# The first pieces of k and q of a rotary-embedding score kernel, split over two DMA rings

## The chip, the cores and the metric

The kernel runs on one core of a Trainium2 chip. The metric is the time of the kernel on the device in microseconds (us), the median of the runs shown. The core has TensorE (PE) for matmuls and transposes, VectorE (DVE) and ScalarE (ACT) for elementwise work, GpSimd (POOL), and SyncE (SP), which in this kernel does nothing but issue transfers. Transfers between the large memory (HBM) and the on-chip memory run on 16 DMA engines. SyncE and ScalarE can both issue them, each into a queue of its own; a DMA issue is an instruction on the issuing engine's queue (written SPq, ACTq, POOLq in the profile), and a semaphore tells when the data has landed.

## The reference

The inputs q and k have the shape (16, 512, 16, 64): batch, position, head, dimension. Both are rotated by position, and then every query of a head is multiplied with every key of the same head and batch:

```python
q_rot = concat([q1 * cos - q2 * sin, q1 * sin + q2 * cos], axis=-1)   # q1, q2: halves of the last axis
k_rot = concat([k1 * cos - k2 * sin, k1 * sin + k2 * cos], axis=-1)
scores = einsum('bshd,bthd->bsht', q_rot, k_rot)                      # (16, 512, 16, 512), float32
```

The inputs are 67 MB, the output is 268 MB.

## The kernel before, in words

A batch has 512 positions; position 4p + c lies in partition p, so that a batch of q or k is a tile of 128 partitions x 4 positions x 16 heads x 64 values, 2 MB, loaded by one DMA (`load`, L122). The kernel walks over 64 steps, four a batch. From batch 1 on, a step is one c: its q tile is rotated on VectorE by `rope` (two products, L149 and L150, and a sum, L154), transposed on TensorE through an identity (L170), copied out of PSUM (L185), and multiplied with the batch's transposed keys (`scores`, L201); ScalarE copies each 128 x 1024 result into a stage tile (L208), and one DMA of 4 MB stores the tile (`store`, L188). There are three stage buffers. The order of all instructions is written out by hand under `tc.manual_schedule()`; each engine's queue runs in program order. Batches are loaded well ahead, and the loads stand in SyncE's queue between the stores.

Batch 0 is treated differently, so that work can begin before 2 MB have landed. It is cut by heads: a step of batch 0 is four heads, with all four c. `load_units` loads pieces of it into a tile named `early`: the first four heads of k, then those of q (512 KB each, runs of 1 KB), then the other twelve heads of k and of q (1536 KB each, runs of 3 KB). Their DMAs are issued at L67. Batch 0's results are stored in pieces of 1 MB (L211).

Before these, ScalarE issues the loads of cos and sin (L225, 64 KB each), and then makes `ss_t` out of sin (L232 and L233: a copy, and a copy times -1). The first instruction of ScalarE proper is a table load, which the profile puts on L232. VectorE's first product (L149) needs the first piece of k and `ss_t`, its second (L150) `cos_t`.

Five later loads (`RELIEVED`) go through GpSimd's queue in another split (`load_around`, L98, L111). They are untouched.

The waits between engines and DMAs are set by the framework. DMAs issued by SyncE and ScalarE take turns on eight semaphores, so the ninth DMA waits, before it is issued, until the first has landed.

Of the kernel before, what the change touches and what calls it, by code (L numbers as in the profile page):

```python
# [10 lines left out]
def kernel(  # L11
# [8 lines left out]
    nc = tc.nc  # L20
# [4 lines left out]
    B, S, H, D = q.shape  # L25
    HD = D // 2
    P = 128
# [3 lines left out]
    G = H // C  # L31
# [27 lines left out]
    units = {}  # L59
    used = [0]  # L60

    def load_units(which, head, heads):
        n = C * heads * D
        t = early[:, used[0] : used[0] + n].rearrange("p (c e) -> p c e", c=C)
        used[0] += n
        src = dram[which][0, :, :, head : head + heads, :]
        nc.sync.dma_start(t.rearrange("p c (h d) -> p c h d", d=D), src)  # L67
        for h in range(0, heads, G):
            units[which, (head + h) // G] = t[:, :, D * h : D * (h + G)]

# [42 lines left out]
    def load(which, b):  # L113

        if b >= B:
            return
        t = in_pool.tile([P, C, H * D], fp32, tag=which + "_in", name=which + "_sb")
        batches[which, b] = t
        if (which, b) in RELIEVED:
            load_around(which, b, t)  # L120
        else:
            nc.sync.dma_start(t.rearrange("p c (h d) -> p c h d", h=H), dram[which][b])  # L122

    def rope(which, n):


        part = part_pool.tile([P, H * D], fp32, tag="part", name="part")
        if n < C:
            x = units[which, n]
            sv, k1, k2 = "p c (g j) -> p c g j", {"j": HD}, {"j": D}  # L130
            cs = cos_t.unsqueeze(2).to_broadcast((P, C, 2 * G, HD))
            ss = ss_v.unsqueeze(2).to_broadcast((P, C, G, D))
            pv = part.rearrange("p (c g j) -> p c g j", c=C, j=D)
            x5 = x.rearrange("p c (h x j) -> p c h x j", x=2, j=HD)
            p5 = part.rearrange("p (c h x j) -> p c h x j", c=C, x=2, j=HD)
            adds = [(x5[:, :, :, y], p5[:, :, :, 1 - y]) for y in range(2)]
        else:
            x = batches[which, n // C][:, n % C]
            sv, k1, k2 = "p (g j) -> p g j", {"j": HD}, {"j": D}
            cs = cos_t[:, n % C].unsqueeze(1).to_broadcast((P, 2 * H, HD))  # L140
            ss = ss_v[:, n % C].unsqueeze(1).to_broadcast((P, H, D))
            pv = part.rearrange(sv, **k2)
            x4 = x.rearrange("p (h x j) -> p h x j", x=2, j=HD)
            swapped = bass.AP(part.tensor, part.offset + HD, [part.ap[0], (D, H), (-HD, 2), (1, HD)])
            adds = [(x4, swapped)]
        xs, xc = x.rearrange(sv, **k2), x.rearrange(sv, **k1)

        def products():
            nc.vector.tensor_tensor(pv, xs, ss, op=mult)  # L149
            nc.vector.tensor_tensor(xc, xc, cs, op=mult)  # L150

        def sums():
            for y, z in adds:
                nc.vector.tensor_tensor(y, y, z, op=add)  # L154

        return [products, sums]
# [33 lines left out]
    def scores(i, p, st):  # L190

        ps = ps_s_pool.tile([P, 2, S], fp32, tag="ps_s", name="ps")
        b = i // C
        if b == 0:
            c, hp = divmod(p, 2)
            lhs, rhs = qT[i][:, C * hp + c], kT[0][:, 2 * i + hp]
        else:
            lhs, rhs = qT[i][:, p], kT[b][:, p]
        for r in range(2):
            po, rh = ps[:, r, :], rhs[64 * r : 64 * r + 64, :]  # L200
            nc.tensor.matmul(  # L201
                out=po, lhsT=lhs[64 * r : 64 * r + 64, :], rhs=rh, start=True, stop=True
            )
        so, si = st[:, 2 * p : 2 * p + 2, :], ps
        if b > 0:
            so = so.rearrange("s r (t c) -> s r t c", c=C)
            si = si.rearrange("s r (c t) -> s r t c", c=C)
        nc.scalar.copy(out=so, in_=si)  # L208
        if b == 0 and p % 2 == 1:
            c = p // 2  # L210
            nc.sync.dma_start(o_v[0, c, :, G * i : G * (i + 1)], st[:, G * c : G * (c + 1)])  # L211
        elif b > 0 and p == HP - 1:
            store(i, st)

    def tr_act(which, n):
        for g in range(2):
            transposed(which, n, g, nc.scalar.copy)

    def run(ops):
        for op in ops:  # L220
            op()

    with tc.manual_schedule():
        for t, src in ((cos_t, cos), (sin_t, sin)):
            nc.scalar.dma_start(t, src.rearrange("(p c) j -> p c j", c=C))  # L225
        for head, heads in ((0, G), (G, H - G)):
            load_units("k", head, heads)
            load_units("q", head, heads)
        load("k", 1)
        load("q", 1)  # L230
        make_identity(nc, ident)
        nc.scalar.copy(out=ss_t[:, :, 0, :], in_=sin_t)  # L232
        nc.scalar.mul(ss_t[:, :, 1, :], sin_t, -1.0)  # L233
        for which in ("k", "q"):
            run(rope(which, 0))
            tr_act(which, 0)


        for i in range(C):
            st = st_first[i] if i < 2 else stage_pool.tile([P, H, S], fp32, tag="stage", name="st")  # L240
            if i < C - 1:
                dve = rope("k", i + 1) + rope("q", i + 1) + rope("k", C + i)
                nxt = [("k", i + 1), ("q", i + 1)]
            else:
                dve = rope("q", C) + rope("k", C + i) + rope("q", C + 1) + rope("k", 2 * C)
                nxt = [("q", C), ("k", C + i)]
            for p in range(HP):
                scores(i, p, st)
                if p in (0, 1) and i > 0:
                    run(dve[:1])  # L250
                    dve = dve[1:]
                    transposed("k", C + i - 1, p, nc.vector.tensor_copy)
                if p == 3 and i < 2:
                    load("kq"[i], 2)
                if p in (2, 6):
                    m = len(dve) - (4 if p == 2 else 2) - (2 if i == C - 1 else 0)
                    run(dve[:m])
                    dve = dve[m:]
                    tr_act(*nxt.pop(0))
            run(dve)  # L260
        load("k", 3)


        for i in range(C, NST):
            tr = {}
            if i + 1 < NST:
                tr[1], tr[3] = ("q", i + 1, 0), ("q", i + 1, 1)
            if i + C < NST:
                tr[5], tr[6] = ("k", i + C, 0), ("k", i + C, 1)
            dve = []  # L270
            if i + 2 < NST:
                dve += rope("q", i + 2)
            if i + 1 + C < NST:
                dve += rope("k", i + 1 + C)
            st = stage_pool.tile([P, H, S], fp32, tag="stage", name="st")
            for p in range(HP):
                scores(i, p, st)
                if p not in tr:
                    continue
                if tr[p][0] == "q":  # L280
                    run(dve[:1])
                    dve = dve[1:]
                    transposed(*tr[p], nc.vector.tensor_copy)
                else:
                    transposed(*tr[p], nc.scalar.copy)
            run(dve)
            if i % C == C - 2:
                load("q", i // C + 2)
            elif i % C == C - 1:
                load("k", i // C + 3)  # L290
# [30 lines left out]
```

## Time and profile before

| | |
|---|---|
| time, median of 3 runs | 792.87 us (792.67 to 793.26) |
| profiled execution | span 790.4 us, from the first to the last instruction; no other time of this execution is given |
| PE, DVE, ACT busy | 684.4 us (87%), 544.7 us (69%), 562.0 us (71%) |
| DMA | 336.18 MB, 425 GB/s over the span; SyncE's queue (q1) 325.46 MB, GpSimd's (q0) 10.10 MB, ScalarE's (q10) 0.13 MB |
| first piece of k, issue to landing | 4.8 us |
| first piece of q, issue to landing | 5.6 us |
| sin, issue to landing | 3.7 us |
| 4 MB stores, issue to landing | 24.7 us (median of 60) |
| mean granted TensorE clock | 0.934 |

An engine's busy time is what its instructions took; issuing a DMA isn't counted as busy. The page's rows of 40 digits cut the span into 40 slices and give the busy share in tenths. The time from issue to landing includes the time in which a transfer stands behind others in its queue. A stretch of time is shown by the trace with the busy time of PE, PE's weight loads, DVE, ACT and POOL in it, then the granted clock, the mean busy share of the 16 DMA engines, and GB/s.

### The profile page before, as it was taken

What the parts mean: (1) busy time and instruction counts of PE and PEld (TensorE: products, weight loads), DVE (VectorE), ACT (ScalarE), POOL (GpSimd) and SP (SyncE); (2) the same over time, 40 slices, a digit from 0 to 9 for tenths busy, and PEclk for the clock granted to TensorE, in tenths of its full rate; (3) what the DMA queues carried; (4) which work ended last, traced back from release to release, by engine and by line L of the source; (5) the groups of instructions that cost most, each with busy time, mean ns of one, the idle gap of its engine ahead of it and who ended that gap; (6) DMA issues with size and microseconds to landing.
All of it is one profiled execution on the core that took longest, in us unless ns stands there. A gap on an engine that the chain in (4) does not pass through costs nothing.

```text
span 790.4 us, 7750 instructions
## 1 busy us (share of the span) xinstructions
PE 684.4 (87%) x3072; PEld 296.4 (38%) x3072; DVE 544.7 (69%) x516; ACT 562.0 (71%) x647; POOL 11.9 (2%) x24
## 2 busy tenths in 40 slices
PE   4989998988988889798996989889899798799960
PEld 2444443433433334343342433334334343344420
DVE  6999988666766678576785767667678487587400
ACT  3888886865857768486785866777577586588770
POOL 0000000000001000000000001000000000000000
PEclk9999999998999999898998989999899899899995
DMA  9999999999999999999999999999999999999997
GB/s 357 417 425 439 429 430 435 425 435 436 429 429 428 413 432 419 433 423 438 433 427 436 426 432 429 422 432 424 430 432 427 436 429 432 430 432 434 432 429 340
DMA packets 18836, 336.18 MB, mean 425 GB/s; under 512 B 2312, under 2 KB 3592, under 8 KB 4616
## 3 DMA queue, kind: packets, MB, share of 16 engines
q1 hardware_dynamic: 16704, 325.46, 96.4%
q0 software_dynamic: 1808, 10.10, 3.1%
q8 instruction: 24, 0.39, 0.2%
q10 hardware_dynamic: 288, 0.13, 0.1%
q14 instruction: 12, 0.10, 0.0%
HBM read 67.24 MB, written 268.44 MB: 425 GB/s over the span
## 4 chain that ended last, share of the span: by engine, by line
DMA 49%; PE 40%; ACT 5%; DVE 3%; issue 1%; ACTq 0%; SPq 0%; DVEq 0%
DMA out_dram<-st 46%; PE ps L201 30%; PE bank L170 10%; ACT st L208 5%; DMA q_sb<-in_q_dram 2%; DVE part L149 1%; DMA early<-in_k_dram 1%; DVE q_sb L150 0%; DVE k_sb L154 0%; DVE k_sb L150 0%; DVE q_sb L154 0%; DVE early L150 0%; DVE kT_t L185 0%; ACTq L316 0%; DVE early L154 0%
## 5 line engine op out<-in xcount | busy, mean ns | idle before, releaser
L208 ACT COPY st<-ps 128x1024 f32<-128x1024 f32 x512 | 495.7, 1020 | 192.6 <-DMA out_dram<-st 109.8
L201 PE MATMUL ps<-kT_t,qT_t 64*128 64x512 f32 x2048 | 544.0, 649 | 67.0 <-ACT st L208 67.0
L201 PEld LDWEIGHTS ps<-kT_t,qT_t 64*128 64x128 f32 x2048 | 183.6, 196 | 256.2 <-issue 133.3
L185 DVE COPY qT_t<-bank 128x512 f32<-128x512 f32 x118 | 81.6, 691 | 193.9 <-PE bank L170 193.9
L170 PEld LDWEIGHTS bank<-ident,q_sb 128*128 128x128 f32 x480 | 54.2, 149 | 99.0 <-issue 96.4
L170 PEld LDWEIGHTS bank<-ident,k_sb 128*128 128x128 f32 x480 | 50.3, 140 | 96.4 <-DVE k_sb L150 39.5
L170 PE MATMUL bank<-ident,q_sb 128*128 128x128 f32 x480 | 85.1, 304 | 0.9 <-PE ps L201 0.9
L170 PE MATMUL bank<-ident,k_sb 128*128 128x128 f32 x480 | 78.5, 286 | 1.6 <-DVE qT_t L185 1.2
L185 ACT COPY kT_t<-bank 128x512 f32<-128x512 f32 x122 | 72.4, 598 | 6.4 <-PE bank L170 6.4
L154 DVE TENSOR_TENSOR k_sb<-k_sb,part 128x1024 f32<-128x1024 f32 x60 | 73.5, 1225 | 2.1
L150 DVE TENSOR_TENSOR q_sb<-q_sb,cos_t 128x1024 f32<-128x1024 f32 x60 | 73.5, 1225 | 2.1
L150 DVE TENSOR_TENSOR k_sb<-k_sb,cos_t 128x1024 f32<-128x1024 f32 x60 | 73.5, 1225 | 2.0
L149 DVE TENSOR_TENSOR part<-q_sb,ss_t 128x1024 f32<-128x1024 f32 x60 | 73.5, 1225 | 2.0
L149 DVE TENSOR_TENSOR part<-k_sb,ss_t 128x1024 f32<-128x1024 f32 x60 | 73.0, 1216 | 0.9 <-DMA k_sb<-in_k_dram 0.7
L154 DVE TENSOR_TENSOR q_sb<-q_sb,part 128x1024 f32<-128x1024 f32 x60 | 72.9, 1216 | 0.0
L170 PE MATMUL bank<-ident,early 128*128 128x128 f32 x64 | 10.5, 315 | 12.4 <-DVE early L154 10.5
L170 PEld LDWEIGHTS bank<-ident,early 128*128 128x128 f32 x64 | 8.3, 161 | 17.4 <-issue 13.4
L149 DVE TENSOR_TENSOR part<-early,ss_t 128x1024 f32<-128x1024 f32 x8 | 9.8, 1222 | 5.8 <-DMA early<-in_k_dram 5.7
L98 POOL DMA_DIRECT2D q_sb<-in_q_dram x3 | 2.3, 752 | 620.2 <-PE bank L170 446.2
L154 DVE TENSOR_TENSOR early<-early,part 128x512 f32<-128x512 f32 x16 | 10.3, 687 | 0.2
L150 DVE TENSOR_TENSOR early<-early,cos_t 128x1024 f32<-128x1024 f32 x8 | 9.8, 1225 | 0.3
L185 ACT COPY qT_t<-bank 128x512 f32<-128x512 f32 x10 | 5.7, 629 | 3.2 <-PE bank L170 3.2
(12 smaller groups left out, 15.9 us busy)
## 6 DMA issues: line engine op xcount, KB each, us to landing
out_dram<-st SPq DMA_DIRECT2D x60, 4096.0 KB, 24.7
k_sb<-in_k_dram SPq DMA_DIRECT2D x13, 2048.0 KB, 28.3
q_sb<-in_q_dram SPq DMA_DIRECT2D x12, 2048.0 KB, 26.5
out_dram<-st SPq DMA_DIRECT2D x16, 1024.0 KB, 13.8
q_sb<-in_q_dram POOLq DMA_DIRECT2D x3, 1920.0 KB, 27.8
k_sb<-in_k_dram POOLq DMA_DIRECT2D x2, 1920.0 KB, 43.3
early<-in_k_dram SPq DMA_DIRECT2D x1, 1536.0 KB
early<-in_q_dram SPq DMA_DIRECT2D x1, 1536.0 KB
```

The source lines that it names most:

```text
L98: nc.gpsimd.dma_start(dst, src)
L149: nc.vector.tensor_tensor(pv, xs, ss, op=mult)
L150: nc.vector.tensor_tensor(xc, xc, cs, op=mult)
L154: nc.vector.tensor_tensor(y, y, z, op=add)
L170: nc.tensor.transpose(bank[:, x, :], src, ident)
L185: copy(out=dst, in_=src)
L201: nc.tensor.matmul(out=po, lhsT=lhs[64 * r : 64 * r + 64, :], rhs=rh, start=True, stop=True)
L208: nc.scalar.copy(out=so, in_=si)
```

## The change

The first pieces of k and of q are each loaded by two DMAs: partitions 0 to 63 by one that SyncE issues, partitions 64 to 127 by one that ScalarE issues. ScalarE's two come after those of cos and sin in its queue. The pieces with the other twelve heads are issued as before, by SyncE alone.

```diff
-    def load_units(which, head, heads):
+    def load_units(which, head, heads, queues):
         n = C * heads * D
         t = early[:, used[0] : used[0] + n].rearrange("p (c e) -> p c e", c=C)
         used[0] += n
         src = dram[which][0, :, :, head : head + heads, :]
-        nc.sync.dma_start(t.rearrange("p c (h d) -> p c h d", d=D), src)
+        dst = t.rearrange("p c (h d) -> p c h d", d=D)
+        m = P // len(queues)
+        for x, queue in enumerate(queues):
+            queue.dma_start(dst[m * x : m * (x + 1)], src[m * x : m * (x + 1)])
...
-        for head, heads in ((0, G), (G, H - G)):
-            load_units("k", head, heads)
-            load_units("q", head, heads)
+        for head, heads, queues in ((0, G, (nc.sync, nc.scalar)), (G, H - G, (nc.sync,))):
+            load_units("k", head, heads, queues)
+            load_units("q", head, heads, queues)
```

## The prediction

> **What bounds the kernel now.** I read the page's summary first, then stretches of the DMA engines over the whole run, then the first twenty microseconds as a timeline.
>
> ```profile
> span 790.4 us, 7750 instructions
> DMA  9999999999999999999999999999999999999997
> HBM read 67.24 MB, written 268.44 MB: 425 GB/s over the span
> DMA 49%; PE 40%; ACT 5%; DVE 3%; issue 1%; ACTq 0%; SPq 0%; DVEq 0%
> ```
>
> The DMA engines are above nine tenths in 39 of 40 slices. The chain that ended last gives PE 40%, but it is a chain that hops between engines running side by side: its long pieces are the 4 MB stores, which take 20 to 31 us from issue to landing, although one store moves in about 9.7 us (4.19 MB at 430 GB/s). Two or three transfers are therefore always queued, and a store that is issued a little earlier only waits longer in the queue. The next view tests that: stretches of time, and at the end of each row the share of the sixteen DMA engines that was busy and the rate.
>
> ```profile
> 1.00:2.00 1.00, 0.00 (x0) 0.00 (x0) 0.00 (x0) 0.37 (x1) 0.59 (x2) 1.00 0.17 49
> 2.00:3.00 1.00, 0.00 (x0) 0.00 (x0) 0.00 (x0) 0.91 (x1) 0.39 (x1) 1.00 0.67 165
> 3.00:4.00 1.00, 0.00 (x0) 0.00 (x0) 0.00 (x0) 0.00 (x0) 0.00 (x0) 1.00 0.81 248
> 4.00:5.00 1.00, 0.00 (x0) 0.00 (x0) 0.00 (x0) 0.08 (x1) 0.00 (x0) 1.00 1.09 362
> 6.00:7.00 1.00, 0.00 (x0) 0.00 (x0) 0.96 (x2) 0.00 (x0) 0.00 (x0) 1.00 1.01 378
> 40.00:780.00 740.00, 655.93 (x2937) 281.43 (x2936) 511.39 (x483) 538.70 (x616) 10.52 (x17) 0.94 1.01 430
> 782.00:784.00 2.00, 0.00 (x0) 0.00 (x0) 0.00 (x0) 0.00 (x0) 0.00 (x0) 0.50 0.83 360
> 784.00:786.00 2.00, 0.00 (x0) 0.00 (x0) 0.00 (x0) 0.00 (x0) 0.00 (x0) 0.50 0.76 328
> 786.00:788.00 2.00, 0.00 (x0) 0.00 (x0) 0.00 (x0) 0.00 (x0) 0.00 (x0) 0.50 0.38 164
> ```
>
> The reader is to see three stretches. Up to about 4 us the engines fill up (0.17, 0.67, 0.81). From 4 to 782 us they are full (1.01; a packet is booked in the slice in which it starts, so values pass 1). From 782 us they run dry at different times. The end of the run is thus the start of the DMA work, plus bytes by rate, plus the uneven last 6 us. Compute has room: in the steady part stores are issued 10.02 us apart while compute sets the pace, and the transfers of one such step (a store, and half a load) need 9.7 + 2.4 = 12.1 us. Only a change in the filling, in the rate, or in the balance of the engines at the end can move the end. Now the start, as a timeline (start, length, engine, line):
>
> ```profile
> 0.74 0.66 SPq L67 DMA_DIRECT2D early<-in_k_dram  x1
> 1.15 0.45 ACTq L225 DMA_DIRECT2D sin_t<-in_sin_dram  x1
> 1.46 0.60 SPq L67 DMA_DIRECT2D early<-in_q_dram  x1
> 1.63 1.28 ACT L232 ACT_TABLE_LOAD   x1 [1.63 <-PEq L305]
> 4.92 0.30 ACT L232 COPY ss_t<-sin_t 128x128 f32<-128x128 f32 x1 [2.00 <-DMA sin_t<-in_sin_dram]
> 5.12 0.30 ACT L233 ACTIVATE ss_t<-sin_t 128x128 f32<-128x128 f32 x1
> 5.67 1.23 DVE L149 TENSOR_TENSOR part<-early,ss_t 128x1024 f32<-128x1024 f32 x1 [5.67 <-DMA early<-in_k_dram]
> 9.52 1.23 DVE L149 TENSOR_TENSOR part<-early,ss_t 128x1024 f32<-128x1024 f32 x1
> 19.52 3.28 SPq L211 DMA_DIRECT2D out_dram<-st  x2
> ```
>
> VectorE's first product starts 0.10 us after k's first piece lands (0.74 + 4.83 = 5.57). The first store goes out at 19.52 us, while the DMA engines are still on reads: batch 1's q, issued at 4.17, lands 20.6 us later, at 24.8.
>
> **The change, part by part.** *Earlier data for VectorE.* Its first product needs ss_t too, ready at 5.12 + 0.30 = 5.42. So k can land early by what it likes: unless sin comes earlier as well, the product moves by at most 5.67 - 5.42 - 0.1, some 0.15 us; sin may come a little earlier, as only half of k stands ahead of it. On the end this is worth nothing. What follows is transposes, scores, the store at 19.52, and that store waits behind reads until 23 to 24.8 us. The cover is these 8 MB of reads; without it, the 0.15 us is all there would be.
>
> *ScalarE.* Two more issues stand between sin's issue and the table load. Issues of 64 KB to 512 KB last 0.38 to 0.66 us, so 0.8 to 1.3 us for two. The table load then ends at 3.7 to 4.2 us instead of 2.91, and its next work waits for sin until 4.92. Cost nothing; with sin landed early, at most the early part is lost. Nothing else is queued on ScalarE before 10.7 us.
>
> *SyncE.* Its two issues become half as large: 0.33 (the shortest DMA issue on SyncE, a 1 MB store) to 0.66 us each, so what follows is issued 0 to 0.6 us earlier. In the built order, batch 1's k now waits for cos to have landed, and batch 1's q for SyncE's half of k, since transfers share eight semaphores in turn and two more came in. The second wait moves q's issue from 4.17 to about 5; behind it on SyncE is only the store of 19.52, and q's transfer starts after 19 us. Nothing. Later the turn is shifted by two, yet each transfer still waits for the eighth before it.
>
> *The filling.* This is the only term that reaches the end. Its best value: 2 to 4 us run at the 378 GB/s of the 6 to 7 us row. The shortfall is (378 - 165) + (378 - 248) = 343 KB, at 430 GB/s 0.80 us. It can't be more, since SyncE's first issue stays at 0.74 and the first packets with it. Its worst value: all of the two pieces (1.05 MB) at the 165 GB/s of the 2 to 3 us row, 6.4 us, where before they and sin took from 2.1 to 6.6 us, 4.5 us: 1.9 us lost. No row shows two rings with such pieces; nearest is 3 to 5 us, where sin on ScalarE's ring runs beside k on SyncE's, and there the rate rises from 248 to 362. From 2 to 3.6 us, k alone on its ring ran slower, so I take a small gain, 0.3 us, a bit under half of the best. The two added completions are 32 records of 9 ns over 16 engines, 0.02 us.
>
> The Trainium skill speaks against the change: "DMA: Bandwidth & Descriptors", section "Rules for kernel authors", says not to split a transfer into partition halves, as both halves use the same sixteen engines. By it the sum would be zero, 792.9. "SBUF — State Buffer", section "Door 1: The DMA port swizzle", says partitions 0 to 63 reach only half of the sixteen ports; by its 435 GB/s, my estimate is that 1.05 MB would take 4.8 instead of 2.4 us if the halves never ran side by side, 2.4 us lost. No row of this trace has a half transfer to show either.
>
> Sum on the profiled execution: 790.4 - 0.3 = 790.1 us. The median of the three runs is 792.87, 2.5 us over the profiled span, which is what lies around it; with that kept, 792.6. A measurement here can tell about 0.2%, 1.6 us, so this is no change.
>
> **The rivals.** *Slower: the half on ScalarE's ring comes late.* It stands behind cos and sin; sin, issued at 1.15, needed 3.75 us for 64 KB. Meanwhile SyncE's ring offers k's and q's large pieces in packets three times as large. At worst the half of k waits for all of the large k piece, which landed at 10.9 us in the trace: 5.3 us late. Compute and the first store shift with it. The point from which it decides: the first of the sixteen engines ends batch 1's q at about 23.5 us, and a DMA needs about 1.4 us from its issue to its first packet (k: 0.74 to 2.1), so the first store, now at 19.52, may go out 2.6 us later before an engine idles. So 5.3 - 2.6 = 2.7 us, 795.6. Against it: k and sin, on two rings, did interleave. Chance 0.12. *Slower: half transfers run at a lower rate,* the bound above, 792.87 + 1.9 = 794.8; 0.05.
>
> *Faster: the engines end more evenly.* The last rows leave 0.17, 0.24 and 0.62 of 2 us unused, 2.1 us. If the split shifts which engine is ahead, the end could come up to 2.1 us earlier, 790.8. Against it: all sixteen engines get the same bytes either way, if 64 rows go four to an engine. That the filling gives all of its 0.8 us (792.1) is still no change by the measure. Chance of a gain over 1.6 us 0.13.
>
> *It does not do what it says*: ScalarE's descriptors could be made only after SyncE's, sin's late packets hint at it; then 792.9. This lies inside the forecast.
>
> **How the numbers follow.** Forecast, no change, 0.70: 791.9 to 794.4 by the two ends of the filling. Faster 0.13, slower 0.12 + 0.05 = 0.17. The range reaches from 791.3, the edge of a gain that can be told, to 795.2, past the rate bound and well into the late half; it leaves out most of the gain (0.12) and some of the late half (0.05), under 2 in 10.
>
> **What would show it.** Right: shares above 0.67 and 0.81 in 2 to 4 us; the first product between 5.3 and 6.5 us; full DMA from 19 to 26 us; the same slope at the end. Wrong: DMA shares under 0.9 from 20 to 30 us (late half), under 0.67 from 2 to 4 us (rate), or another run-out from 782 us on (balance).

## The result and the profile after

The changed kernel takes 796.59 us (median of 5 runs, 795.0 to 796.96), the kernel before 792.87 us (5 runs, 792.47 to 793.26): a ratio of 1.0041, with a 95% interval of 1.0029 to 1.0054. It is 3.7 us slower, outside the predicted range of 791.3 to 795.2. The profiled execution of the changed kernel has a time of 796.01 us, 1.8 us over its span; its span is 3.8 us longer than that of before.

From the page: the span, the rate over it, and the group of VectorE's first products of batch 0 (busy time, mean ns, idle time before it and what ended that).

```profile
span 794.2 us, 7755 instructions
HBM read 67.24 MB, written 268.44 MB: 423 GB/s over the span
L152 DVE TENSOR_TENSOR part<-early,ss_t 128x1024 f32<-128x1024 f32 x8 | 9.8, 1222 | 9.0 <-DMA early<-in_k_dram 8.8
```

The bytes are the same, the rate over the span fell from 425 to 423 GB/s, and VectorE now waits 8.8 us for k's first piece, 5.7 us before. Stretches of the changed kernel; the last two columns are the mean busy share of the DMA engines and GB/s:

```profile
2.00:3.00 1.00, 0.00 (x0) 0.00 (x0) 0.00 (x0) 0.00 (x0) 0.41 (x1) 1.00 0.55 149
3.00:4.00 1.00, 0.00 (x0) 0.00 (x0) 0.00 (x0) 0.97 (x1) 0.00 (x0) 1.00 1.24 239
4.00:5.00 1.00, 0.00 (x0) 0.00 (x0) 0.00 (x0) 0.61 (x3) 0.00 (x0) 1.00 0.60 161
6.00:7.00 1.00, 0.00 (x0) 0.00 (x0) 0.00 (x0) 0.00 (x0) 0.00 (x0) 1.00 1.11 267
34.00:36.00 2.00, 2.00 (x16) 1.22 (x14) 1.97 (x3) 1.50 (x3) 0.00 (x0) 1.00 1.13 303
40.00:780.00 740.00, 659.52 (x2958) 282.98 (x2956) 515.32 (x486) 540.45 (x620) 10.53 (x17) 0.94 1.01 430
786.00:788.00 2.00, 0.00 (x0) 0.00 (x0) 0.00 (x0) 0.00 (x0) 0.00 (x0) 0.50 0.76 328
788.00:790.00 2.00, 0.00 (x0) 0.00 (x0) 0.00 (x0) 0.00 (x0) 0.00 (x0) 0.50 0.57 246
790.00:792.00 2.00, 0.00 (x0) 0.00 (x0) 0.00 (x0) 0.00 (x0) 0.00 (x0) 0.50 0.31 131
```

Three things are to be seen. The row of 3 to 4 us books more busy time than before (1.24 against 0.81) and moves fewer bytes (239 against 248 GB/s); the 0.60 of the next row is the other side of it, as a packet is booked in the slice in which it starts. From 6 to 7 us it is 1.11 at 267, before 1.01 at 378. So the engines are not short of work, their packets take longer. The same thing comes back at 34 to 36 us (1.13 at 303), long after the split pieces. In the kernel before that row is

```profile
34.00:36.00 2.00, 2.00 (x14) 1.07 (x14) 1.97 (x2) 2.00 (x4) 0.00 (x0) 1.00 0.98 406
```

And the 740 us of the steady part have the same rate, 430 GB/s. The loss is made in the first 40 us, and the run-out ends some 4 us later. Now the start as a timeline:

```profile
1.65 0.62 ACTq L70 DMA_DIRECT2D early<-in_k_dram  x1
2.30 0.70 ACTq L70 DMA_DIRECT2D early<-in_q_dram  x1
3.03 1.28 ACT L235 ACT_TABLE_LOAD   x1 [3.03 <-issue]
4.71 0.30 ACT L235 COPY ss_t<-sin_t 128x128 f32<-128x128 f32 x1 [0.39 <-DMA sin_t<-in_sin_dram]
8.78 1.22 DVE L152 TENSOR_TENSOR part<-early,ss_t 128x1024 f32<-128x1024 f32 x1 [8.78 <-DMA early<-in_k_dram]
23.37 3.70 SPq L214 DMA_DIRECT2D out_dram<-st  x2
```

SyncE's half of k landed at 4.60 us, ScalarE's at 8.65: the late half sets the first product (8.78, before 5.67), and the first store goes out at 23.37 instead of 19.52. ScalarE's half of q is as late: it landed at 12.60 (the whole piece before at 7.03), and VectorE's first product of q started at 12.72, before at 9.52. With k on time, q would have held compute up by nearly as much.

To place the loss, I summed the bytes of all packets up to a given moment, subtracted what the trace of before had moved by then, and divided by the steady 430 GB/s. The changed kernel is 1.57 us behind at 10 us, 1.99 at 18, 1.75 at 26, 3.24 at 40 and 3.28 at 780. There are two losses, **2.0 us by 18 us and 1.5 us between 26 and 40 us**; the remaining half microsecond of the 3.8 arises in the run-out. Behind each is a packet time. A packet of 1 KB takes 46 to 47 ns on average before (4 to 6 us), and 60 to 72 ns on ScalarE's ring after (5 to 10 us); packets of 3 KB take 121 to 141 ns before, and after 165 to 191 ns until 9 us and 144 to 155 until 12. Between 28.5 and 36.5 us the 8 KB packets of the stores (309 ns elsewhere) take up to 436 ns, and the 16 KB packets of the loads (611 ns elsewhere) up to 1192 ns, as means of half a microsecond.

### The profile page after: what moved, and what is told of

Same layout as the page of the kernel before. It is cut to its first block, busy times and chain, and to the rows that moved or that the text cites. A ratio compares the mean times of both kernels' runs of the same rounds, so it can differ in the third digit from the quotient of the medians.

```text
span 794.2 us, 7755 instructions
## 1 busy us (share of the span) xinstructions
PE 684.8 (86%) x3072; PEld 296.4 (37%) x3072; DVE 544.5 (69%) x516; ACT 561.6 (71%) x647; POOL 11.9 (2%) x24
## 3 DMA queue, kind: packets, MB, share of 16 engines
q0 software_dynamic: 1808, 10.10, 3.0%
## 4 chain that ended last, share of the span: by engine, by line
DMA 49%; PE 37%; DVE 6%; ACT 5%; issue 1%; ACTq 0%; DVEq 0%
DMA out_dram<-st 48%; PE ps L204 28%; PE bank L173 9%; ACT st L211 5%; DVE part L152 2%; DMA early<-in_k_dram 1%; DVE early L157 1%; DVE k_sb L157 1%; DVE k_sb L153 1%; DVE early L153 1%; DVE kT_t L188 0%; DVE q_sb L153 0%; DVE q_sb L157 0%; ACTq L319 0%; ACTq L228 0%
```

## The experiments

Two theories were held against each other: that half transfers move slower (RATE), and that compute, and the first stores with it, becomes late (LATE). Ratios are to the kernel before on the same chip. "Behind" is the sum above, in us at 430 GB/s; a "landing" is a time in the span.

**The changed kernel again.** r1_again and r10_again are the changed kernel without an edit.

> The changed kernel once more, against the kernel before on the same chip. Two theories stand. RATE: the half transfers, or the two rings in turn, slow the DMA engines from 3 to 12 us, which puts them about 2.0 us behind. LATE: ScalarE's half of k lands 3.1 us later, the first store goes out at 23.4 instead of 19.5, and the slow stretch at 29 to 38 us (1.25 us) follows from it. If both are regular, this profile has them again: 2.0 us behind at 18 us, some 3.2 us at 40 us, a time of 796 to 797. If the second stretch was an accident of one execution, this profile ends near 792.4 with a time near 795.

> One more execution of the changed kernel, to see its trace. Its two traces so far differ by one thing: the slow stretch at 29 to 37 us was in the one of 796.0 us (first store 23.4, k's second half landed at 8.65) and not in the one of 794.5 us (22.2 and 7.8). If a late first store brings the stretch on, this execution has it when its first store goes out after about 22.5 us, and its time is then near 796 and otherwise near 794.7.

r1_again: 795.65 us over 8 runs, ratio 1.0033 [1.0023, 1.0043]. Its profiled execution took 794.47 us, the lowest of the eight, and was behind by 1.47 us at 10 us and 1.88 at 18, but only 1.63 at 40 and 1.74 at 780: the first loss was there, the second was not. ScalarE's half of k landed at 7.76 us, and the first store went out at 22.19. VectorE waited for the late half of q as well, so that TensorE began its first scores at nearly the same time as in the traced change. Two lines of r1_again, then one of the traced change:

```profile
12.60 1.22 DVE L152 TENSOR_TENSOR part<-early,ss_t 128x1024 f32<-128x1024 f32 x1 [0.90 <-DMA early<-in_q_dram]
18.39 3.52 PE L204 MATMUL ps<-kT_t,qT_t 64*128 64x512 f32 x12
```

```profile
18.50 5.06 PE L204 MATMUL ps<-kT_t,qT_t 64*128 64x512 f32 x12
```

The same twelve matmuls took 3.52 us here and 5.06 us there. Most of the difference in the first two stores (issued at 22.19 and 25.07 here, at 23.37 and 26.73 there) is TensorE's pace and not the half of k. The granted clock reads 1.00 in both stretches, and these runs do not show what sets the pace.

r10_again (one execution, 796.37 us) was behind by 1.80 at 10 and had no slow stretch at 26 to 40 us either, although its store was as late as 22.88; it lost another 1.5 us between 10 and 26 us, where its 16 KB load packets took 680 instead of 611 ns. That third loss I cannot explain. So the first loss is in all three traces of the changed kernel, the second in one; how many of the untraced runs have it is not known.

**What makes the halves slow.** Both halves on SyncE's ring, then alternate partitions instead of halves:

```diff
-(0, G, (nc.sync, nc.scalar))
+(0, G, (nc.sync, nc.sync))            # r2, and r5 too
...
-dst[m * x : m * (x + 1)], src[m * x : m * (x + 1)]
+dst[x::m], src[x::m]                  # r5 alone, with m = len(queues)
```

> Both halves of k and of q are issued by SyncE, one after the other; ScalarE issues only cos and sin. RATE by half transfers (sixteen engines writing the same 64 partitions): the engines fall behind before 8 us as in the changed kernel, by 1 to 2 us, time 794 to 795. RATE by two rings: nothing is lost, 792.9. LATE: k's second half lands near 5.6 to 6.5 us, the first store at 19.5 to 20.5, no second stretch, so nothing from there.

> As the run with both halves on SyncE, but the halves are the even and the odd partitions, so that each transfer of 64 partitions reaches all of the tile's partition range. That run had lost 1.36 us by 9 us and 1.3 us of bytes at 40 us. RATE by location (all sixteen engines writing into partitions 0 to 63): nothing lost, the bytes at 18 us within 0.3 us of the kernel before, time as before. RATE by the shape of 64 rows (how such a transfer is made into descriptors, or its issue): 1.3 us lost again, time 0.1 to 0.15% over the kernel before.

r2: 794.36 us, 1.0013 [1.0004, 1.0021]. r5: 794.37 us, 1.0014 [1.0006, 1.0023]. Equal times, but not for the same reason. Stretches of r2, then of r5:

```profile
4.00:5.00 1.00, 0.00 (x0) 0.00 (x0) 0.00 (x0) 0.04 (x1) 0.00 (x0) 1.00 1.12 218
5.00:6.00 1.00, 0.00 (x0) 0.00 (x0) 0.00 (x0) 0.47 (x2) 0.00 (x0) 1.00 0.88 198
```

```profile
4.00:5.00 1.00, 0.00 (x0) 0.00 (x0) 0.01 (x1) 0.51 (x2) 0.00 (x0) 1.00 0.86 280
6.00:7.00 1.00, 0.00 (x0) 0.00 (x0) 0.97 (x2) 0.00 (x0) 0.00 (x0) 1.00 0.72 200
```

In r2 the engines are booked full and move 218 and 198 GB/s; packets of 1 KB take 67 to 82 ns. That is the slow rate with one ring and nothing late on another, so the second ring isn't needed for it: 1.36 us behind at 10 us. In r5 the packets take 49 to 52 ns, near the 47 of before, and the engines are short of work (0.86, 0.72): each issue of 64 rows takes 0.6 to 0.7 us, as long as one of 128 rows, so the two large pieces, issued from 2.11 us on before, come from 3.49 us on, and it is 0.88 us behind at 10 us. By its time alone (0.14% over the kernel before) r5 would speak for the shape of 64 rows; the packets say otherwise. Its trace is the lowest of its twelve times, 793.27 us, so what its median loses beyond this is not traced; r2's trace, 794.56 us, is near its median. The number of rows is the same in both; **which partitions lie in one transfer sets the packet time.** Neighbouring partitions hold neighbouring rows of HBM, so these runs do not separate the side that is written from the side that is read.

Next a split that keeps all 128 partitions in each transfer: by position, on both rings, for k and q (r3) and for k alone (r8). And the first change with ScalarE's halves ahead of cos and sin (r7).

```diff
-m = P // len(queues); dst[m * x : m * (x + 1)], src[m * x : m * (x + 1)]
+m = C // len(queues); dst[:, m * x : m * (x + 1)], src[:, m * x : m * (x + 1)]   # r3, r8
...
+load_units("q", head, heads, queues[:1])                                        # r8: q whole, on SyncE
...
+if head == 0: cos and sin are loaded here, after ScalarE's halves               # r7, halves of 64 partitions
```

> The same two rings and the same bytes on each, but cut by position: SyncE takes the first two of the four positions, ScalarE the last two, both with all 128 partitions. RATE by half transfers: packets stay at 46 ns (1 KB) and 122 ns (3 KB), nothing is lost before 18 us. RATE by two rings: about 2 us behind at 18 us, as in the changed kernel. LATE: ScalarE's part of k lands near 8.6 us again, the first store at 23 us, and the second stretch (about 1.2 us) is there; time 794 to 796.6.

> Only k's first piece is split, by position (all 128 partitions), over SyncE and ScalarE; q's is whole on SyncE. With both pieces split so, k landed at 5.4 us, q at 10.0, and the first store went out at 20.75. LATE: k at about 5.3 us, q at 6.5 to 7.5 us, first store at 19.3 to 19.8 us, no time lost there. RATE: no half transfer, nothing lost; the filling may gain 0.2 to 0.4 us. Time within 0.05% of the kernel before.

> The changed kernel with ScalarE's two halves issued before cos and sin instead of after. LATE by the place in the queue: ScalarE's half of k lands near 5 us as SyncE's does, sin lands later, near 6 to 7 us, and the first product starts near 7 us instead of 8.8; the first store near 21.3 us. RATE by half transfers stays in part: the two rings write into different halves at the same time, so the loss before 9 us falls from 1.3 to under 0.7 us. Time 0.05 to 0.2% over the kernel before.

r3: 795.9 us, 1.0032 [1.002, 1.0045]; its profiled execution was the lowest of six, 793.65 us. A stretch of it:

```profile
4.00:5.00 1.00, 0.00 (x0) 0.00 (x0) 0.00 (x0) 0.51 (x2) 0.00 (x0) 1.00 1.07 329
```

Packets of 1 KB take 46 ns in the median on both rings, and it was 0.21 us behind at 10 us: no slow rate, though two rings share the engines. Yet its median is 2.6 us over before. What that is, r11 and r12 below show. r8: 793.68 us, 1.0014 [0.9999, 1.0029] (twelve runs, one of them 799.34), no gain; its first product came at 6.63 us, later than before, since ScalarE's half of k landed at 6.51. r7: 798.05 us, 1.0059 [1.0046, 1.0073], the worst. I had expected it to mend the late half. ScalarE's half did land at 5.51, but sin, now behind it in the ring, landed only at 11.33, and the first product came at 11.90: the same lateness by another operand. It was 1.02 us behind at 18 us and 4.88 at 40.

**What lateness costs by itself.** In the kernel before, VectorE makes its first product of batch 0 several times over (the same result), each time 1.23 us; nothing is changed in any load.

```diff
+for _ in range(3 if which == "k" and n == 0 else 0):    # r4; 2 in r6, 1 in r9
+    nc.vector.tensor_tensor(pv, xs, ss, op=mult)
```

> The kernel before with VectorE's first product of k done four times instead of once, so that all compute of the first piece starts 3.7 us later, and no transfer is changed. LATE: the first store goes out near 23.3 us, the DMA engines lose 1 to 1.5 us between 25 and 40 us, time about 794.2. RATE: the engines were never behind at 18 us, reads cover the delay, time 792.9.

> The kernel before with VectorE's first product of k done three times, so that compute starts 2.5 us later; with four times (3.7 us later) the first store went out at 23.8 us and the engines lost 3.6 us. LATE with slack: first store near 22.5 us, close to where the fastest engine runs dry, at most 0.3 us lost, time within 0.05% of the kernel before. LATE without slack: 2 us or more lost, 0.25% slower.

> The kernel before with VectorE's first product of k done twice: compute starts 1.25 us later, the first store goes out near 20.8 to 21.2 us. With 2.5 us (store at 22.6) 2.2 us were lost between 26 and 36 us, most of it with busy engines and packets of up to twice the usual time. LATE as a threshold: nothing lost in most executions, ratio under 1.001. LATE by degrees: about 1 us, ratio 1.001 to 1.0015.

| delay of VectorE | first store | behind at 18 / 26 / 40 us | time of the traced execution | median, ratio |
|---|---|---|---|---|
| none (before) | 19.52 | 0 | not given | 792.87 |
| 1.25 us (r9) | 20.58 | -0.23 / -0.45 / -0.21 | 792.86 | 793.8, 1.0011 [1.0, 1.0021] |
| 2.5 us (r6) | 22.62 | -0.09 / -0.17 / 2.24 | 795.56 | 795.56, 1.003 [1.0021, 1.004] |
| 3.7 us (r4) | 23.84 | -0.22 / 0.92 / 3.67 | 796.98 | 795.74, 1.0036 [1.0023, 1.0049] |

The runs were on three chips, on which the kernel before had medians of 793.0 to 793.3 us.

LATE alone costs about as much as the whole change (1.003 and 1.0036 against 1.0041 and 1.0033). In the traces it is a step and not a slope: 1.25 us of delay lost nothing, 2.5 us lost 2.4 us between 26 and 40 us. The times do not show the step: r9's trace is the second lowest of its eleven times, and its ratio, 1.0011, lies where LATE by degrees had it. Stretches of r4, then one of r6:

```profile
26.00:28.00 2.00, 2.00 (x12) 0.87 (x10) 1.97 (x2) 1.91 (x4) 0.00 (x0) 1.00 0.52 217
34.00:36.00 2.00, 2.00 (x14) 1.07 (x14) 1.97 (x4) 1.37 (x3) 0.00 (x0) 1.00 1.05 279
```

```profile
34.00:36.00 2.00, 2.00 (x11) 0.95 (x11) 1.93 (x3) 1.91 (x4) 0.00 (x0) 1.00 0.78 254
```

In r4 the engines are half idle at 26 to 28 us (0.52), between the first store and the second, and before the first store's packets, from 23 to 25 us, an engine was idle for 1.4 us on average. That was expected. What was not: afterwards, with work queued and 1.05 booked, they move 279 GB/s, as in the changed kernel. In r6 the 8 KB packets take up to 596 ns (at 28.5 to 29.5 us) and the 16 KB packets up to 1236 ns (at 33.5 us). Counted over the time that its packets take, r6's row of 34 to 36 us is 1.00 busy, not the 0.78 that is booked. So the slow stretch needs no split piece; a first store that comes late brings it about.

r11_positions_again and r12_positions_again are two more executions of r3's kernel, to see whether one kernel shows both cases.

> One more execution of the split by positions. Its traced execution took 793.7 us with nothing lost before 40 us, but its median was 795.9. LATE: in the slow ones ScalarE's half of q lands after 10 us, the first store goes out after 22 us, and the slow stretch of 1.5 to 2 us lies between 26 and 37 us. If the time is over 795 and there is no such stretch, the cause lies elsewhere.

> The same as the run before it in this list, once more, since single executions of this kernel differ by 2 us: over 795 us with a first store after 22 us and a slow stretch between 26 and 37 us, or near 793.7 without.

r11 took 794.79 us, with its first store issued at 22.70 us; r12 took 793.29 us, with it at 20.49. Two stretches of r11, then the same of r12:

```profile
28.00:30.00 2.00, 2.00 (x11) 0.65 (x9) 1.97 (x2) 2.00 (x4) 0.00 (x0) 1.00 1.07 332
34.00:36.00 2.00, 2.00 (x12) 1.02 (x12) 1.93 (x3) 1.91 (x4) 0.00 (x0) 1.00 0.72 233
```

```profile
28.00:30.00 2.00, 2.00 (x14) 0.91 (x12) 2.00 (x4) 1.43 (x3) 0.00 (x0) 1.00 1.10 467
34.00:36.00 2.00, 2.00 (x13) 0.77 (x10) 1.97 (x3) 2.00 (x4) 0.00 (x0) 1.00 1.01 418
```

Same kernel: with the store at 22.70 the slow stretch is there (332 and 233 GB/s, 2.35 us behind at 40 us), with the store at 20.49 it isn't (467 and 418 GB/s, 0.13 behind). Of the 2.21 us between the two stores 1.36 come from ScalarE's half of k, which landed at 8.28 us in r11 and at 6.92 in r12, and most of the rest from TensorE, whose first twelve score matmuls took 4.43 and 3.53 us. In r3 the half of k landed at 5.37, but VectorE's product of q had to wait for its half until 10.10, the matmuls took 4.83 us, and the store went out at 20.75.

The issue of the first store alone does not decide (r1_again: 22.19, r10_again: 22.88, no stretch). What goes with the loss in all fourteen traces up to here, before included, is how much of store 1 is left when store 2 is issued; this measure was chosen after these traces had been seen. I took the time from store 2's issue to the first of store 1's sixteen completions. Where it is 1.2 us or less, 1.5 to 2.8 us are lost between 26 and 40 us (the traced change 1.19, r7 0.77, r11 0.72, r6 0.70, r4 0.33). Where it is 1.98 us or more, at most 0.3 us (before 3.84, r10_again 3.85, r2 3.91, r5 4.33, r1_again 2.73, r8 2.67, r12 2.59, r9 2.34, r3 1.98). The three traces of the next experiment have 5.5 to 7.3 us and lose nothing at 26 to 40 us. With idle engines a store's first packet came 0.85 us after its issue (r4: 23.84 to 24.70), so at 1.2 us or less hardly anything of store 1 is left when store 2's packets arrive. That is not the same as idle engines: counted from the packets in flight at 22 to 30 us, an engine idled 2.2 us on average in r4, 2.0 in r7, 0.5 in r6, 0.2 in r11 and 0.01 in the traced change, where never fewer than 15 of 16 were at work, as in the kernel before. Idle time is a part of the loss and not all of it: from 18 to 40 us r4 and r7 lost 3.9 us, r6 2.3, r11 1.9 and the traced change 1.2; without the idle time 1.2 to 1.9 us stay in each of the five. So a queue that is about to run out goes with the loss. The changed kernel's slow start helps it here: in r1_again and r10_again the queue was itself 1.6 and 3.3 us late at 26 us, and lasted longer. In the traced change it was 1.75 us late, much as in r1_again; between these two the second store's issue decided, and with it TensorE's pace.

**Can the thin place be filled?** Batch 2's k is loaded right after batch 1's q, so that 2 MB more stand in the queue when the first stores come; in the changed kernel (r13), in r6 (r14) and in the kernel before (r15).

```diff
 load("q", 1)
+load("k", 2)
...
-if p == 3 and i < 2: load("kq"[i], 2)
+if p == 3 and i == 1: load("q", 2)
```

> The changed kernel with batch 2's k (2 MB) issued right after batch 1's q, ahead of the first store, so that the reads cover about 5 us more. Queue running dry as the cause of the second loss: no slow stretch in any execution, what stays is the 1.4 to 2.0 us of the half transfers, time near 794.6, ratio 1.002. Late compute as such: the stretch stays in about half of the executions, ratio 1.003 to 1.004.

> Compute 2.5 us late as in the run that lost 2.2 us at 26 to 36 us (ratio 1.003), with batch 2's k issued ahead of the first store. Queue running dry: the whole loss goes, time within 0.3 us of the kernel before. Late compute as such: 2 us lost still.

> The kernel before with batch 2's k issued ahead of the first store and nothing else changed. Queue running dry: the kernel before keeps 3.8 us from its second store to the end of its first in the profiled execution, so nothing is gained in the usual execution; only its slowest ones (over 794.5 us) could come down. Ratio 0.999 to 1.0005.

r15: 793.04 us, 1.0003 [0.9994, 1.0011], nothing. r13: 796.77 us, 1.0039 [1.0025, 1.0053]; r14: 795.12 us, 1.0025 [1.0014, 1.0035]. Neither gained what I expected: r13 has the ratio that late compute as such had been given (1.003 to 1.004), and r14, 2.05 us over the kernel before, has its 2 us. In r14 the stretch at 26 to 40 us is indeed gone, and comes back later. Two stretches of r14, then the second one in the kernel before:

```profile
34.00:36.00 2.00, 2.00 (x11) 0.91 (x11) 1.93 (x3) 1.91 (x4) 0.00 (x0) 1.00 1.02 430
106.00:114.00 8.00, 8.00 (x40) 3.31 (x36) 6.57 (x8) 6.90 (x8) 0.00 (x0) 1.00 0.99 328
```

```profile
106.00:114.00 8.00, 8.00 (x42) 3.37 (x38) 7.18 (x7) 7.12 (x9) 0.00 (x0) 1.00 1.01 432
```

r14 is at -0.30 us at 40 us, 0.39 at 100, 2.25 at 120; r15, with the same loads and no delay, is at -0.33, -0.28 and 0.31. From 73 to 104 us three steps have no load beside them; compute needs 10.02 us for each and a store moves in 9.7, so the queue thins, the engines fall short at each store (shares of 0.93, 0.92 and 0.90 in the 2 us slices at 76, 86 and 96 us, with each packet counted over the time that it takes; 1.01, 1.00 and 1.00 before), and then 16 KB packets take 805 and 943 ns (110 to 112 and 112 to 114 us). As far as this trace shows, the loss was moved to the next thin place, not taken away. In r13's traced execution (795.59 us) 2.0 us are lost at the start and 0.6 at 104 to 116 us, where r15 loses as much; why its median is 1.2 us longer was not traced. So that a filled queue takes the second loss away is shown for the stretch of 26 to 40 us, and not for the time.

No version tried beats the kernel before.

## Why the prediction was wrong

*The filling* failed, and with its sign: "I take a small gain, 0.3 us". The first loss measured 1.4 to 2.0 us in the traces of the changed kernel (1.47, 1.57 and 1.80 us at 10 us; 1.88 and 1.99 at 18, and 2.76 in r10_again with its unexplained reads). The term's worst end, 1.9 us, was right as a size by luck, as it was worked out from a row of the start-up; the fault was the choice of the nearest row. I took rows where two rings share the engines with transfers of all partitions, and r3 shows that those are at 46 ns a packet. What changed the rate was the location of 64 neighbouring partitions, for which no row existed. r2 attributes 1.4 us to it; the other 0.6 us, in the changed kernel alone, fall where ScalarE's halves still run beside the 3 KB packets. That these are the cause is argued, not shown.

The two rules that I quoted stood on opposite sides. "SBUF — State Buffer", section "Door 1: The DMA port swizzle", lets 64 neighbouring partitions reach half of the ports; half of its 435 GB/s is 218, and r2's rows have 218 and 198. My estimate by it, 2.4 us lost, was nearer than my row. "DMA: Bandwidth & Descriptors", section "Rules for kernel authors", is right that the split brings nothing, but the sum by it, zero, is 1.4 to 2.0 us short.

*The half on ScalarE's ring comes late*, at 0.12, came true as described: its k landed 3.1, 2.2 and 2.6 us after the 5.57 of before. It left out q, whose half, landing at 12.5 to 12.9 us in the three traces, would alone have made compute some 3 us late. Its price failed. "The first store ... may go out 2.6 us later before an engine idles. So 5.3 - 2.6 = 2.7 us" takes the slack at the first store and charges what goes beyond it. By that the traced change, with its store 3.85 us later, loses 1.25 us, and r6, with 3.1, loses 0.5 us; they lost 1.5 and 2.4. Its 1.4 us to the first packet were those of a load; a store's came after 0.85 us. In these traces the place that decided was the second store: it follows 2.9 to 3.4 us after the first, which moves in 2.45 us (1.05 MB at 430 GB/s), so once the reads are through the engines run dry between the two (in r6 0.5 us an engine, most of it there). And the price is more than the idle time: 1.2 to 1.9 us come on top of it, in the traced change, with 0.01 us of idle time, all of it as slow packets.

With both terms as measured the sum closes, as it must, since its terms are differences between the two traces: 790.4 + 2.0 - 0.2 (18 to 26 us) + 1.5 + 0.5 (run-out) = 794.2, the span. Without the second loss it would be some 792.7, the span that r1_again has.

"Compute has room" held for the steps with loads beside them (12.1 us of transfers for 10.02 of compute) and not for 73 to 104 us, as r14 shows. I read the mean step and not the thinnest.

Two sums of the prediction are off without changing its outcome. The ends of the filling give 792.1 to 794.8, as in its rivals, not 791.9 to 794.4. And the 2.5 us between the median and the profiled span are not what lies around a span: in every run that lists both this is 1.7 to 1.8 us, so the profiled execution of before took about 792.2 us, less than the median.

Right were these. *Earlier data for VectorE* is worth nothing, as far as r5 shows it: its first product came at 4.99 us, its store at 19.14, and it gained nothing, though it also lost 0.9 us in the filling. *ScalarE*'s two issues took 0.62 and 0.70 us, the table load ended at 4.31 (just past the 3.7 to 4.2), and its next work began at 4.71, when sin had come. *SyncE*'s wait put q's issue at 4.63, and nothing followed from it. The rate of the steady part is the same, and the engines do not end more evenly: that rival, my 0.13 for faster, is not in any trace. The three signs named for wrong appeared in part: 0.55 under 0.67 at 2 to 3 us (rate); the late half showed in the first product at 8.78, outside 5.3 to 6.5, and in a rate of 390 GB/s from 20 to 40 us (419 before), while the DMA shares stayed at 0.92 to 1.05 from 20 to 30 us, which I had named as the sign that would fall.

## What to carry to other kernels

Where a load has to be split, keep all partitions in each transfer (here by position, which kept the packets at 46 ns, though no split gained anything), and read GB/s beside the share of busy engines, since slow packets book as busy. In this kernel, bound by DMA, the slack of an early delay was set at the thinnest places of the queue downstream (two small stores in a row, steps without loads), so each such place has to be measured, from one issue to the completions before it. A queue at that edge cost 1.2 to 1.9 us more than its idle time, so a lateness is priced by an experiment that only delays compute, and by more than one trace of it.

## What the runs showed of the hardware that was not expected

After a moment in which the DMA queue was all but empty, later packets took up to twice as long for some microseconds (in r6 596 instead of 309 ns for 8 KB and 1236 instead of 611 ns for 16 KB, as means of half a microsecond), with the engines busy all the time. Some seven microseconds can lie between that moment and the worst packets (r6: idle at 26 us, the worst 8 KB packets at 29, the worst 16 KB packets at 33.5). The mechanism is open: idle engines are not needed (the traced change), and whether it depends on the sixteen engines having come into step was not tried.

An issue of 64 rows in four runs each takes as long (0.59 to 0.72 us) as one of 128 rows in four runs each (0.60 to 0.66 us), while 128 rows in two runs each, the same number of runs as the first, take 0.43 to 0.49 us. In these traces halving the partitions did not shorten an issue, and halving the runs did.

TensorE's first twelve score matmuls, the same work in every run, took 3.48 us (r7) to 5.06 us (the traced change), with a granted clock of 1.00 in the profile; by that alone the first stores move by more than a microsecond. These runs do not show what sets it.

The order of landing on a ring that shares the engines with another varies between executions: the same half of k landed at 5.37, 6.92 and 8.28 us in three executions of r3's kernel. What sets it is open, as are r10_again's 16 KB load packets of 680 ns, from 15 to 27 us.
